# Spreading the loads of u's rows over time and fixing SyncE's order in the stage of u

## The chip, the cores and the metric

The kernel runs on one core of a Trainium2 chip. The metric is the device time of one execution in microseconds (us), lower is better. It is given as the median of several runs; beside it stands one execution that was recorded by the hardware profiler, with the times of every instruction and DMA.

Engines are named as in the profile: PE (matmul), DVE (VectorE), ACT (ScalarE), POOL (GpSimd) and SP (SyncE, which here does nothing but issue DMAs). Each works through its own instructions in order.

## The reference

One layer of a streaming encoder, on a sequence of 1024 tokens with 1024 channels, all in float32. The case lies in its first sub-layer, where the normalised input is projected into q, k, v, u and two gates, and u goes through a state-space branch:

```python
h = rms_norm(x, norm_mix_pre[l])
proj = h @ w_in[l]
q, k, v, u, gate_logits = jnp.split(proj, splits, axis=-1)
gate_attn, gate_ssm = jnp.split(jax.nn.sigmoid(gate_logits + b_gate[l]), 2, axis=-1)
o_attn = stick_breaking_attention(q, k, v)
o_ssm = s5_branch(u, ssm_a_re[l], ssm_a_im[l], ssm_log_dt[l], ...)
merged = gate_attn * (o_attn @ w_branch_attn[l]) + gate_ssm * (o_ssm @ w_branch_ssm[l])
x = x + rms_norm(merged @ w_out[l], norm_mix_post[l])
...
```

In `s5_branch` the 512 channels of u form 32 groups of 16, each with 64 complex states, and a linear recurrence runs over the 1024 tokens. Behind the first sub-layer come a cross-attention into 256 memory tokens and a gated feed-forward layer with a short convolution; they are the larger part of the kernel and the change doesn't touch them.

## The kernel before

**Precision.** A float32 matmul is made of three: each operand is split into a high part (a cast on ACT) and a low part (the difference). `mm3` (lines 143 to 145) multiplies high by high, high by low and low by high, so line 145 needs the low part of the weights.

**An order by hand.** From line 223 on, the first sub-layer is written against an own clock in us: `at(t, go)` puts a piece of work into a heap, and `all_events` runs the heap in order of time. The instructions of PE, ACT, DVE and POOL are emitted under `manual_schedule`, so each of these four engines has exactly that order. SP is not among them: its DMAs are placed by the scheduler of the tile framework, which is free to issue one before others that were written ahead of it.

**Semaphores of SP's DMAs.** The framework deals eight semaphores in turn to the DMAs of SP. A DMA waits until the one eight places before it has landed, so at most eight are under way. A wait is made by SP before it issues, and everything behind in its queue stands still meanwhile.

**The stage of u.** `channels` computes u transposed in four blocks b of 128 channels, each in two halves h of 512 tokens. DVE scales each half into the tile `ut` (line 482), and after the second half SP writes it to DRAM (`u_d`, line 484). The scan needs u with eight successive tokens and 16 channels on the 128 partitions, so the block is read back by eight small DMAs, one for each m, into 16 partitions of the tile `U` (line 488, 64 KB each). Before the change, all eight stand in one event, 4.0 behind the block's last matmul.

**The scan steps.** Then eight steps n run, `SLOT` = 12.2 apart; step n reads u's block n // 2. `states` is a matmul with `U` (line 766) and a chain on DVE (lines 775 to 787) that ends with `rc`; `outputs` multiplies `U` with the table `Tt` (line 800) and `rc` with `F1` (line 801). `Tt` has one buffer, and each block's entries are spread into it by eight DMAs from `ktt` (line 742). ACT applies the GELU to the sum (line 806). `tables` (lines 694 to 703) makes sines and cosines for a block: a memset on POOL, sums on DVE, then three activations on ACT.

**The filler.** Between these small pieces PE works on gate projections (`gate_job`, 16 steps of three matmuls for each). Their weights come by `Job.weights`: SP loads `ws` (line 253, two buffers), ACT casts it to `wh` (line 257), and the low part is either a difference on DVE (line 261, first job) or, from the second job on, made by ACT writing -`ws` into `wl` (line 265) and a DMA of POOL's queue that adds the weights from DRAM (line 266). A result half is copied by ACT into `glog` (line 295), which has one buffer in this stage, and SP writes it to DRAM (`g_d`, line 296). ACT can't copy the next half until that write has landed.

`u_begin` and `u_end` are the times of the plan at which the stage of u begins and at which the last matmuls of u end; `in_line` doesn't exist yet.

Of the kernel before, what the change touches and what calls it, by code (L numbers as in the profile page):

```python
# [20 lines left out]
P = 128  # L21
# [24 lines left out]
def kernel(ctx: ExitStack, tc: tile.TileContext, a: dict, out: bass.AP, dbg=None):  # L46
    nc = tc.nc
    V, G, C, T = nc.vector, nc.gpsimd, nc.scalar, nc.tensor
    dma = nc.sync.dma_start
# [7 lines left out]
    u_d = dpool.tile([512, 8, P], F32, name="u_d")  # L57
# [45 lines left out]
    def ps(tag):  # L103
        pool, w, n = psum[tag]
        return pool.tile([P, w], F32, tag=tag, name="ps_" + tag, bufs=n)
# [36 lines left out]
    def mm3(acc, sh, sl, mh, ml, first, last):  # L142
        T.matmul(acc, sh, mh, start=first, stop=False)  # L143
        T.matmul(acc, sh, ml, start=False, stop=False)  # L144
        T.matmul(acc, sl, mh, start=False, stop=last)  # L145
# [80 lines left out]
    STEP = 0.70  # L226
    events, seen = [], []

    def at(t, go):
        heapq.heappush(events, (t, len(seen), go))  # L230
        seen.append(t)
# [12 lines left out]
    class Job:  # L244
# [6 lines left out]
        def load(self, t):  # L251
            self.ws = wpool.tile([P, 1024], F32, tag="ws", name="ws", bufs=WS)
            dma(self.ws[:, :self.n], self.src)
# [90 lines left out]
    def h_hi(k, sl):  # L344
        return hT[0][k // 4][:, k % 4, sl]

    def h_lo(k, sl):
        return hT[1][k // 4][:, k % 4, sl]
# [16 lines left out]
    U = pa.tile([P, 32, P], F32, name="U")  # L365
# [97 lines left out]
        at(now + STEP + 7.0, put)  # L463

    ut = {}

    def channels(now, b, h, k):

        if k == 0:
            accs_[b, h] = ps("m")  # L470
        acc = accs_[b, h]
        ws = slice((k % 2) * 512 + b * P, (k % 2) * 512 + (b + 1) * P)
        wh, wl = (w[:, ws] for w in pair[1, k // 2])
        sl = slice(h * 512, (h + 1) * 512)
        mm3(acc, wh, wl, h_hi(k, sl), h_lo(k, sl), k == 0, k == KT - 1)
        if k < KT - 1:
            return

        def put(t):
            if h == 0:  # L480
                ut[b] = px.tile([P, 8, P], F32, tag="wr", name="ut", bufs=4)
            V.tensor_tensor(ut[b][:, :, 64 * h:64 * h + 64], acc.rearrange("p (j m) -> p m j", m=8), row_u[:, h], op=ALU.mult)
            if h:
                dma(u_d[b * P:(b + 1) * P], ut[b])

        def load(t):
            for m in range(8):
                dma(U[16 * m:16 * m + 16, 8 * b:8 * b + 8], u_d[b * P:(b + 1) * P, m].rearrange("(g c) j -> c g j", c=16))

        at(now + STEP + 0.2 + (1.4 if (b, h) == (0, 0) else 0.0), put)  # L490
        if h:
            at(now + STEP + 4.0, load)

    line(0.0, (lambda: x_load(0, 0), 0), (lambda: dma(gcol, a["g_cols"]), 0), (lambda: w_load(0, 0), 0),
         (lambda: x_load(1, 0), 0), (lambda: w_load(0, 1), 0), (lambda: dma(sp, a["ssm_p"]), 0), (lambda: x_load(0, 1), 0),
# [26 lines left out]
    def begin_of(t):  # L522
        return FIRST + 16 * STEP + 8 * STEP * (t - 2)

    u_begin = begin_of(KT)
# [314 lines left out]
    for t in range(2, KT):  # L840
        last_v = clock
        for k in range(KT):
            pe(STEP, tokens, 0, t, k)
    at(u_begin + 8.0, lambda _: open_t())
    steady = [lambda t, b=b, h=h, k=k: channels(t, b, h, k) for b in range(4) for h in range(2) for k in range(KT)]
    u_begin = clock
    for c in range(4):
# [3 lines left out]
    u_end = u_begin + 64 * STEP + 4.0  # L851
# [44 lines left out]
    def plan(t, took, go, n):  # L896
        heapq.heappush(timed, (t, len(seen), took, go, n))
        seen.append(t)

    plan(u_begin + 27.0, 1.75, intra, 0)  # L900
    plan(u_end - 8.0, 0.45, flip_w, 0)
    plan(u_end - 6.5, 0.45, flip_w, 1)
    plan(u_begin + 1.3, 0.15, lambda now, n: rows_of_rates(now, rates_x[:, 0], KT, rx_d, 0), 0)
# [4 lines left out]
    while timed:  # L908
        t0, _, took, go, n = heapq.heappop(timed)
# [51 lines left out]
    def glu_job(m):  # L961
        def out(t, h, sl, acc):
            def put(t):
                if h == 0:
                    og[m] = open_g.pool.tile([P, S], F32, tag="og", name="og", bufs=2)
                C.activation(og[m][:, sl], acc, AF.Sigmoid, bias=bglu[:, m:m + 1])

            def gated(t):
                V.tensor_tensor(og[m][:, sl], og[m][:, sl], yT[m][:, sl], op=ALU.mult)
                if h:  # L970
                    dma(os_d[m], og[m])

            at(t, put)
            at(t + 0.8, gated)

        return Job(a["w_glu_T"][m], out, n=512, steps=4, operand=lambda k, sl: (yh[k][:, sl], yl[k][:, sl]))

    clock = max(clock, g0_ + 5.2)
    for m in range(4):
        j = glu_job(m)  # L980
# [165 lines left out]
    t, nf, begun, last_z = 0.0, 0, {}, 1e9  # L1146
# [393 lines left out]
    for n, (ch, go, args, last) in enumerate(steady):  # L1540
        while timed and timed[0][0] <= clock + STEP / 2:
            _, _, took, turn_, x = heapq.heappop(timed)
# [17 lines left out]
    while timed:  # L1560
        _, _, took, turn_, x = heapq.heappop(timed)
# [1022 lines left out]
```

## Time and profile before

| | |
|---|---|
| median of 3 runs | 1646.17 us (1645.4 to 1646.4) |
| the profiled execution | 1641.96 us |
| its span, first to last instruction | 1640.2 us |
| mean granted TensorE clock | 0.998 |
| DMA, whole span | 287.13 MB, mean 175 GB/s |

The page gives each engine's busy time over the span. Its time line gives, for every instruction, start, duration, engine, line, operation and operands; in brackets stands how long the engine was idle before it, and what ended the idle time. A matmul is busy longer than it holds up the next one, since matmuls overlap, so the pace of PE is read from the starts. For SP a row is the issue of a DMA, which ends long before the data have landed.

### The profile page before, as it was taken

Reading aid. Unit: us, or ns where it says so; the run is one execution under the profiler, and the core shown is the slowest. Engines: PE = TensorE matmul, PEld = TensorE weight load, DVE = VectorE, ACT = ScalarE, POOL = GpSimd, SP = SyncE. Lnnn points to the kernel's source line nnn. Section 1 sums busy time; section 2 is a strip of 40 time slices with the busy share of each in tenths; the row PEclk is TensorE's granted clock in tenths of the full one; section 3 lists DMA queues with packets and bytes.
Section 4 is the critical chain, followed back from the end, with each engine's and each line's share of the span. In section 5 each row is a group of like instructions: output and inputs, shape, how many; then the busy total and the mean of one; then the engine's idle time right before and its main releaser. Section 6 shows DMA issues by size and latency. Waiting matters only on the chain.

```text
span 1640.2 us, 22339 instructions
## 1 busy us (share of the span) xinstructions
PE 1619.7 (99%) x7996; PEld 1361.3 (83%) x7996; DVE 1161.3 (71%) x1613; ACT 877.6 (54%) x1450; POOL 212.1 (13%) x307
## 2 busy tenths in 40 slices
PE   9999999999999999999999999999999999999998
PEld 7888888888888888888888888888888888888886
DVE  7888637676866688467555678988877888775473
ACT  5416346676766544345444556655555565654441
POOL 5000003333332000011000011111111111000010
PEclk9999999999999999999999999999999999999999
DMA  9444343232424954464413575777776767688571
GB/s 333 163 106 128 98 155 96 65 103 84 125 85 139 335 188 135 167 219 154 141 65 129 206 256 195 220 221 206 198 201 188 203 187 193 205 321 276 194 243 77
DMA packets 130340, 287.13 MB, mean 175 GB/s; under 512 B 22954, under 2 KB 31668, under 8 KB 130100
## 3 DMA queue, kind: packets, MB, share of 16 engines
q1 hardware_dynamic: 116644, 255.02, 46.2%
q0 software_dynamic: 10224, 21.24, 7.3%
q10 hardware_dynamic: 3360, 9.44, 1.5%
q8 instruction: 63, 1.03, 0.3%
q14 instruction: 49, 0.40, 0.1%
HBM read 209.74 MB, written 69.47 MB: 170 GB/s over the span
## 4 chain that ended last, share of the span: by engine, by line
PE 88%; issue 4%; DVE 3%; DMA 2%; ACT 2%; POOL 0%; SPq 0%; ACTq 0%; DVEq 0%; POOLq 0%
PE ps_p L1957 8%; PE ps_p L1958 8%; PE ps_p L1956 8%; PE ps_f L143 6%; PE ps_f L145 6%; PE ps_f L144 6%; PE ps_d L2429 4%; PE ps_d L2430 4%; PE ps_d L2431 4%; PE ps_m L143 3%; PE ps_m L144 3%; PE ps_m L145 3%; PE ps_o L1103 2%; PE ps_w L1078 2%; PE ps_z L143 1%
## 5 line engine op out<-in xcount | busy, mean ns | idle before, releaser
L143 PE MATMUL ps_f<-hT,wh 128*128 128x512 f32 x384 | 161.2, 420 | 0.0
L145 PE MATMUL ps_f<-hT,wl 128*128 128x512 f32 x384 | 150.9, 393 | 1.6 <-DMA wl<-in_w_in_T 1.6
L144 PE MATMUL ps_f<-hT,wh 128*128 128x512 f32 x384 | 150.6, 392 | 0.0
L1958 PE MATMUL ps_p<-qS,bm 128*128 128x512 f32 (+2 forms) x360 | 138.9, 386 | 0.6 <-DVE bm L2162 0.6
L1956 PE MATMUL ps_p<-qS,bm 128*128 128x512 f32 (+2 forms) x360 | 139.0, 386 | 0.1
L1957 PE MATMUL ps_p<-qS,bm 128*128 128x512 f32 (+2 forms) x360 | 138.8, 386 | 0.1
L149 DVE TENSOR_TENSOR dn<-raw,dn 128x1024 fp32r<-128x1024 f32 x77 | 93.4, 1223 | 62.9 <-ACT dn L148 60.2
L148 ACT CAST dn<-raw 128x1024 fp32r<-128x1024 f32 x77 | 80.5, 1054 | 87.1 <-PE ps_d L2431 38.0
L2429 PE MATMUL ps_d<-dn 128*128 128x512 f32 x308 | 119.8, 389 | 0.0
L2430 PE MATMUL ps_d<-dn 128*128 128x512 f32 x308 | 119.8, 389 | 0.0
L2431 PE MATMUL ps_d<-dn 128*128 128x512 f32 x308 | 119.8, 389 | 0.0
L1064 POOL TENSOR_TENSOR s<-s,s 128x127 f32<-128x127 f32 (+4 forms) x96 | 90.0, 938 | 220.3 <-DVE s L1058 175.0
L1957 PE MATMUL ps_p<-qA,bm 128*128 128x512 f32 (+2 forms) x272 | 104.5, 384 | 0.0
L1956 PE MATMUL ps_p<-qA,bm 128*128 128x512 f32 (+2 forms) x272 | 104.5, 384 | 0.0
L1958 PE MATMUL ps_p<-qA,bm 128*128 128x512 f32 (+2 forms) x272 | 104.5, 384 | 0.0
L1973 ACT COPY uu<-ps_p 128x512 f32<-128x512 f32 (+2 forms) x90 | 51.5, 573 | 93.0 <-PE ps_p L1958 93.0
L1902 POOL DMA_DIRECT2D bm<-in_ffn_up_T x61 | 53.5, 876 | 349.7 <-ACT bm L1901 168.5
L145 PEld LDWEIGHTS ps_f<-hT,wl 128*128 128x128 f32 x384 | 72.1, 188 | 18.2 <-DMA wl<-in_w_in_T 2.1
L1052 ACT ACTIVATE s<-ps_z,rates_x 128x128 f32<-128x128 f32 (+3 forms) x96 | 56.3, 587 | 53.6 <-PE ps_z L1041 48.1
L1958 PEld LDWEIGHTS ps_p<-qS,bm 128*128 128x128 f32 x360 | 67.6, 188 | 14.6 <-DVE bm L2162 1.2
L1956 PEld LDWEIGHTS ps_p<-qS,bm 128*128 128x128 f32 x360 | 67.6, 188 | 14.1 <-issue 0.8
L1957 PEld LDWEIGHTS ps_p<-qS,bm 128*128 128x128 f32 x360 | 67.6, 188 | 13.6 <-DVE qS L1784 0.2
(584 smaller groups left out, 4422.6 us busy)
## 6 DMA issues: line engine op xcount, KB each, us to landing
raw<-sd SPq DMA_DIRECT2D x77, 256.0 KB, 3.8
bm<-in_ffn_up_T POOLq DMA_DIRECT2D x61, 256.0 KB, 5.4
ws<-in_w_in_T SPq DMA_DIRECT2D x24, 512.0 KB, 3.6
ws<-in_xa_wo_N SPq DMA_DIRECT2D x23, 512.0 KB, 4.0
wv<-in_ffn_up_T SPq DMA_DIRECT2D x22, 512.0 KB, 4.0
dr<-in_ffn_down SPq DMA_DIRECT2D x22, 512.0 KB, 6.7
td<-st SPq DMA_DIRECT2D x44, 256.0 KB, 5.6
sd<-st SPq DMA_DIRECT2D x44, 256.0 KB, 3.4
```

The lines of the kernel that those rows point to most:

```text
L143: T.matmul(acc, sh, mh, start=first, stop=False)
L144: T.matmul(acc, sh, ml, start=False, stop=False)
L145: T.matmul(acc, sl, mh, start=False, stop=last)
L148: C.copy(dh, src)
L149: (lo or V).tensor_tensor(dl, src, f(dh), op=ALU.subtract)
L1064: G.tensor_tensor(s1[:, n0:e], s1[:, n0:e], s2[:, n0 + 1:e + 1], op=ALU.mult)
L1956: T.matmul(acc, bm[:, 0, ks], q[:, 0, k, cols], start=alone and k == 0, stop=False, skip_group_check=True)
L1957: T.matmul(acc, bm[:, 0, ks], q[:, 1, k, cols], start=False, stop=False, skip_group_check=True)
L1958: T.matmul(acc, bm[:, 1, ks], q[:, 0, k, cols], start=False, stop=k == 3, skip_group_check=True)
L2429: T.matmul(acc[i], v[:, 0, 0, sl], v[:, 0, 1], start=first, stop=False, skip_group_check=True)
L2430: T.matmul(acc[i], v[:, 0, 0, sl], v[:, 1, 1], start=False, stop=False, skip_group_check=True)
L2431: T.matmul(acc[i], v[:, 1, 0, sl], v[:, 0, 1], start=False, stop=last, skip_group_check=True)
```

## The change

The eight loads of a block are now eight events. A table, `LOAD_U`, gives for each block the time of the first one and the distance between them: 0.9, 1.2 and 2.0 us for the first three blocks, and for the last one 3.0 us, starting 16 us behind its matmuls. From 2 us behind `u_begin` to 44 us behind `u_end`, SP is put under `manual_schedule` as well, so in that stretch it issues its DMAs in the order in which they are written down.

```diff
     ut = {}
+    LOAD_U = (4.5, 0.9), (4.5, 1.2), (4.5, 2.0), (16.0, 3.0)
...
-        def load(t):
-            for m in range(8):
-                dma(U[16 * m:16 * m + 16, 8 * b:8 * b + 8], u_d[b * P:(b + 1) * P, m].rearrange("(g c) j -> c g j", c=16))
+        def load(t, m):
+            dma(U[16 * m:16 * m + 16, 8 * b:8 * b + 8], u_d[b * P:(b + 1) * P, m].rearrange("(g c) j -> c g j", c=16))
...
         if h:
-            at(now + STEP + 4.0, load)
+            for m in range(8):
+                at(now + STEP + LOAD_U[b][0] + LOAD_U[b][1] * m, lambda t, m=m: load(t, m))
...
     plan(u_begin + 27.0, 1.75, intra, 0)
+    in_line = ExitStack()
+    at(u_begin + 2.0, lambda _: in_line.enter_context(tc.manual_schedule(engines={mybir.EngineType.SP})))
+    at(u_end + 44.0, lambda _: in_line.close())
```

On PE, ACT, DVE and POOL every instruction stands where it stood. On SP the order changes between the last writes of v and the third spread of `Tt`; nothing is added or left out there. Three places matter. Line numbers of the changed kernel are up to four higher.

The first is SP's queue around the write of u's last block (`u_d<-ut`), the first spread of `Tt` and the first write of a gate half (`g_d<-glog`). Before, from that write of `u_d` on:

```order
L484 DMA u_d<-ut 128x1024
L488 DMA U<-u_d 16x8x128 x8
L742 DMA Tt<-ktt 16x128
L742 DMA Tt<-ktt 32x128
L742 DMA Tt<-ktt 48x128
L742 DMA Tt<-ktt 64x128
L742 DMA Tt<-ktt 80x128
L742 DMA Tt<-ktt 96x128
L742 DMA Tt<-ktt 112x128
L742 DMA Tt<-ktt 128x128
L488 DMA U<-u_d 16x8x128 x8
L296 DMA g_d<-glog 128x512
```

And now, from the same write:

```order
L485 DMA u_d<-ut 128x1024
L488 DMA U<-u_d 16x8x128
L743 DMA Tt<-ktt 16x128
L743 DMA Tt<-ktt 32x128
L743 DMA Tt<-ktt 48x128
L743 DMA Tt<-ktt 64x128
L743 DMA Tt<-ktt 80x128
L743 DMA Tt<-ktt 96x128
L743 DMA Tt<-ktt 112x128
L743 DMA Tt<-ktt 128x128
L488 DMA U<-u_d 16x8x128 x2
L296 DMA g_d<-glog 128x512
```

One load of u stands ahead of `Tt` in place of eight, and three ahead of the write of `g_d` in place of sixteen.

The second place is SP's queue from the last writes of v through the first blocks of u, where the weights of the first two gate jobs (`ws<-in_w_in_T`) are loaded. Before:

```order
L461 DMA v_d<-vr 128x512
L253 DMA ws<-in_w_in_T 128x1024 x2
L461 DMA v_d<-vr 128x512 x2
L423 DMA rx_d<-row_k 8x128
L461 DMA v_d<-vr 128x512
L425 DMA U<-rx_d 128x1024
L484 DMA u_d<-ut 128x1024
L488 DMA U<-u_d 16x8x128 x8
```

Now these two loads stand behind the second and the third write of `u_d`; the rows begin at the second:

```order
L485 DMA u_d<-ut 128x1024
L488 DMA U<-u_d 16x8x128 x7
L253 DMA ws<-in_w_in_T 128x1024
L488 DMA U<-u_d 16x8x128
L485 DMA u_d<-ut 128x1024
L423 DMA rm_d<-row_k 2x128
L488 DMA U<-u_d 16x8x128
L253 DMA ws<-in_w_in_T 128x1024
L488 DMA U<-u_d 16x8x128 x3
```

The first of the two has moved behind seven loads of u's second block, the second behind the write of the third block and its first load.

The third place is SP's queue from the reload of `row_k` on, with the weights of the third job and of those behind it. Before:

```order
L286 DMA row_k<-rx_d 128x512
L253 DMA ws<-in_w_in_T 128x1024
L296 DMA g_d<-glog 128x512
L253 DMA ws<-in_w_in_T 128x1024
L296 DMA g_d<-glog 128x512
L253 DMA ws<-in_w_in_T 128x1024
L742 DMA Tt<-ktt 16x128
```

And now:

```order
L286 DMA row_k<-rx_d 128x512
L296 DMA g_d<-glog 128x512
L253 DMA ws<-in_w_in_T 128x1024
L488 DMA U<-u_d 16x8x128 x3
L296 DMA g_d<-glog 128x512
L488 DMA U<-u_d 16x8x128 x2
L253 DMA ws<-in_w_in_T 128x1024
L743 DMA Tt<-ktt 16x128
```

The third job's load has moved behind the second write of `g_d`, the fourth job's behind the third, and the fifth job's behind the second spread of `Tt`, which is out of these rows.

## Prediction, made before the changed kernel ran

> **What bounds the kernel now.** I read the page first: its head and the engines' busy time.
>
> ```profile
> span 1640.2 us, 22339 instructions
> PE 1619.7 (99%) x7996; PEld 1361.3 (83%) x7996; DVE 1161.3 (71%) x1613; ACT 877.6 (54%) x1450; POOL 212.1 (13%) x307
> ```
>
> PE is idle for 1640.2 - 1619.7 = 20.5 us of the whole span. The change adds and removes no arithmetic, so all it can give is some of these 20.5 us. The second view is PE's waits, cut to 60 to 240 us, the stretch in which the moved transfers run.
>
> ```profile
> PE ps_f L145 <- DMA wl<-in_w_in_T: 1.6, 1, 1.6
> PE ps_m L800 <- issue: 0.4, 1, 0.4
> ```
>
> There are two waits in it. The time line of PE shows them, with neighbours that give the normal pace and the times used further down. A row is start, duration, engine, line, operation.
>
> ```profile
> 112.40 0.39 PE L145 MATMUL ps_f<-hT,wl 128*128 128x512 f32 x1
> ...
> 115.12 0.39 PE L145 MATMUL ps_f<-hT,wl 128*128 128x512 f32 x1
> 115.92 0.46 PE L800 MATMUL ps_m<-Tt,U 128*128 128x128 f32 x2 [0.41 <-issue]
> ...
> 117.56 0.39 PE L801 MATMUL ps_m<-F,rc 128*128 128x128 f32 x2
> ...
> 123.02 0.39 PE L145 MATMUL ps_f<-hT,wl 128*128 128x512 f32 x1
> ...
> 133.41 0.40 PE L144 MATMUL ps_f<-hT,wh 128*128 128x512 f32 x1
> 135.45 0.50 PE L145 MATMUL ps_f<-hT,wl 128*128 128x512 f32 x1 [1.64 <-DMA wl<-in_w_in_T]
> ...
> 142.83 0.39 PE L801 MATMUL ps_m<-F,rc 128*128 128x128 f32 x2
> ```
>
> One matmul takes 0.39 us but the next starts 0.23 us after it (112.40 to 115.12 is twelve such steps of 0.227). So line 800 would have started at 115.12 + 0.23 = 115.35 and started at 115.92: **0.57 us lost**. Line 145 would have started at 133.41 + 0.23 = 133.64 and started at 135.45: **1.81 us lost**. The idle figures in the brackets (0.41 and 1.64, 2.05 together) leave out the overlap of two matmuls; by starts it is 2.38.
>
> What made them late is SP's queue, which issues in order. Its time line:
>
> ```profile
> 43.34 0.94 SPq L253 DMA_DIRECT2D ws<-in_w_in_T  x2
> ...
> 81.50 3.64 SPq L488 DMA_DIRECT2D U<-u_d  x8
> ...
> 91.45 0.34 SPq L484 DMA_DIRECT2D u_d<-ut  x1
> ...
> 101.76 0.34 SPq L484 DMA_DIRECT2D u_d<-ut  x1
> 102.19 6.81 SPq L488 DMA_DIRECT2D U<-u_d  x8
> 109.10 5.08 SPq L742 DMA_DIRECT2D Tt<-ktt  x8
> 114.22 3.90 SPq L488 DMA_DIRECT2D U<-u_d  x8
> 118.22 0.38 SPq L296 DMA_DIRECT2D g_d<-glog  x1
> ...
> 119.11 0.45 SPq L253 DMA_DIRECT2D ws<-in_w_in_T  x1
> ```
>
> Three bursts of eight stand in a row. The eight of Tt start at 109.10, behind eight of U, and are out at 109.10 + 5.08 = 114.18; line 800 waits for them. The first write of g_d waits behind all 24, until 118.22. It holds the only buffer of glog, and ACT needs that buffer back:
>
> ```profile
> 98.08 1.06 ACT L257 CAST wh<-ws 128x1024 fp32r<-128x1024 f32 x1 [0.32 <-PE ps_m L144]
> ...
> 121.46 0.59 ACT L295 COPY glog<-ps_f 128x512 f32<-128x512 f32 x1 [14.40 <-DMA g_d<-glog]
> ...
> 126.31 0.60 ACT L806 ACTIVATE y<-ps_m 128x512 f32<-128x512 f32 x1
> ...
> 127.74 0.59 ACT L295 COPY glog<-ps_f 128x512 f32<-128x512 f32 x1
> 128.21 1.07 ACT L265 ACTIVATE wl<-ws 128x1024 fp32r<-128x1024 f32 x1
> ```
>
> ACT stands still for 14.40 us and then works off its queue; the wl of the third gate job is ready at 128.21 + 1.07 = 129.28. Only then can POOL issue the transfer that adds to it:
>
> ```profile
> 100.41 1.06 POOL L266 DMA_DIRECT2D wl<-in_w_in_T  x1 [5.29 <-ACT wl L265]
> ...
> 129.59 0.88 POOL L266 DMA_DIRECT2D wl<-in_w_in_T  x1 [27.92 <-DVE F L725]
> ```
>
> It lands 5.8 us later, and PE has waited from 133.64.
>
> **The change part by part.** No instruction of PE, ACT, DVE or POOL changes place. SP issues the same DMAs in another order. I need times from issue to landing: minimum, median and maximum by tile (wl from 95 to 150 us, ws from 40 to 150, g_d from 100 to 150), then the one u_d write issued in the quiet stretch from 90 to 100 and the one from 95 to 150:
>
> ```profile
> DMA to landing us min/median/max: 5.3/5.8/7.9
> ...
> DMA to landing us min/median/max: 4.1/4.9/5.7
> ...
> DMA to landing us min/median/max: 2.0/3.1/3.5
> ...
> u_d<-ut SPq DMA_DIRECT2D x1, 512.0 KB, 2.6
> ...
> u_d<-ut SPq DMA_DIRECT2D x1, 512.0 KB, 5.4
> ```
>
> *Tt earlier.* Behind the u_d write at 101.76 stands now one load of U, then the eight of Tt. At the 5.08 / 8 = 0.635 us that each took, they are issued from 102.6 to 107.7; each DMA also waits for the one eight places before it, and for the seventh that is the u_d write itself, landed at 104.4 to 107.2. So all eight are out by 107.0 to 108.5. Line 800 wants them at 115.35 and was 0.57 late with 114.18: over 5 us earlier is enough. The **0.57 us go**. Its partner, line 801, needs rc, which the DVE rows below give at 113.75 + 0.69 = 114.44, still in time.
>
> *g_d earlier.* Two loads of U follow, then the first g_d write, at 108.3 to 109.3, landing after 2.0 to 3.5: 110.3 to 112.8. The second half of the first gate job ends on PE at 112.40 + 0.39 = 112.79. So ACT's second glog copy waits for PE alone, at about 112.8 in place of 121.46. Before, 4.85 us lay between this copy and line 806 (121.46 to 126.31), so line 806 comes at 117.7; its input, the group of line 800, is there at 117.56 + 0.39 - 0.57 = 117.4. The ws of the third job is issued behind the second g_d write, at 114.0 in place of 119.11, and lands at 118.1 to 119.7. wh then ends at 119.2 to 120.7. The third glog copy waits for PE: 123.02 + 0.39 - 0.57 = 122.8. wl follows, from 123.4 to 124.5; POOL issues at 124.8 (0.31 behind ACT, as before) and the landing is at 130.1 to 132.7. PE now wants it at 133.64 - 0.57 = 133.07. Even the longest landing fits, so the **1.81 us go**.
>
> *Two weight loads later.* The ws of the first two gate jobs were issued at 43.34, far ahead. The first now stands behind seven loads of u's second block, at 81.50 + 3.64 = 85.1 at the latest. ACT's cast of it lies before the one of 98.08: it ended at 98.08 - 0.32 = 97.76 and began 1.06 earlier, at 96.7; 85.1 + 5.7 = 90.8 is in time. The second stands behind the u_d write of 91.45 and one load: 91.45 + 2.6 + 0.5 = 94.6, landing at 98.7 to 100.3. ACT's cast, at 98.08 before, moves to 98.7 to 100.3, the POOL transfer of 100.41 to 101.0 to 102.6, and it lands by 110.5 at worst; PE wants it three steps behind 112.40, at 113.1. But a memset of x stands behind it on POOL, and DVE's table work behind that:
>
> ```profile
> 101.64 2.37 DVE L697 TENSOR_TENSOR x<-x,turns 128x8 f32<-128x8 f32 x7
> ...
> 107.37 0.69 DVE L775 TENSOR_TENSOR bp<-ps_m,cosT 128x512 f32<-128x512 f32 x1 [1.36 <-PE ps_m L766]
> ...
> 113.75 0.69 DVE L787 TENSOR_TENSOR rc<-rc,bt 128x508 f32<-128x508 f32 x1
> ...
> 128.76 0.69 DVE L725 TENSOR_TENSOR F<-F,tq 128x512 f32<-128x512 f32 x1
> 130.62 2.38 DVE L697 TENSOR_TENSOR x<-x,turns 128x8 f32<-128x8 f32 x7 [1.17 <-POOL rc L783]
> ...
> 134.91 0.68 DVE L775 TENSOR_TENSOR bp<-ps_m,cosT 128x512 f32<-128x512 f32 x1
> ...
> 141.28 0.69 DVE L787 TENSOR_TENSOR rc<-rc,bt 128x508 f32<-128x508 f32 x1
> ```
>
> DVE has 1.36 us to spare before bp, and rc is 115.35 + 0.23 - 114.44 = 1.1 us early for line 801. A delay of up to 2.5 us is covered; mine is 0.6 to 2.2. Cost: **nothing**, and 1 us for 1 us beyond a cast at 100.5.
>
> *What is late next.* The second wait of DVE for POOL (1.17 at 130.62) goes as well, since POOL's queue is free sooner, and all before it comes 0.57 earlier: x at 128.9, bp 4.29 behind, rc 6.37 + 0.69 behind that: 140.2. Line 801 wants rc at 142.83 - 2.38 = 140.45. That is the tightest spot, 0.2 us to spare; between nothing and 0.3 us could come back here, and I take nothing. The loads of u's last block, now spread behind the second block's Tt loads, are out eleven issues of 0.635 behind 133.41 at the latest, at 140.4; the scan step that reads them is four steps of 12.2 (SLOT in the kernel) behind the one of 134.91, at 183. The Tt loads of the second block wait for PE's last read of Tt, before and after, so they move with PE.
>
> **Sum.** 0.57 + 1.81 = 2.38 us (2.05 by idle time alone). The profiled execution took 1641.96 us, 1640.2 of span and 1.8 around it: 1639.6. The runs have a median of 1646.17, 4.2 above that one execution; I take the same difference off: **1643.8 us**, 0.14% faster, which is under the 0.2% (3.3 us) that a measurement of this kernel can tell from no change.
>
> **The rivals.**
> *The second wait stays.* The row of 129.59 names DVE's F, not ACT, as what released POOL. If POOL truly waits for DVE there, wl is issued at about 129 as before and only 0.57 goes: 1645.6. Against it: at 100.41, where POOL's row names ACT, ACT's product ends 1.07 behind the cast of 98.08 + 1.06, at 100.2, and POOL issues 0.2 later; here it issues 0.31 behind ACT's end, about the same. The Trainium skill, page "SBUF — State Buffer", section "SBUF: two separate sides", states that a transfer issued by GpSimd can be held while VectorE runs an operation in a two-port mode, since the descriptors cannot be written then. By that rule the time would be this rival's, 1645.6. The same page's section "Who interferes with whom" gives the tensor_tensor form, which F is, no such mode, so the row bears the rule out poorly. Other ways of being late by over 0.4 us on that chain end between 1644 and 1645.6. Chance together 0.12.
> *Slower: the second weight load becomes the wait.* It now starts behind a u_d write. If that write lands like the busy one (5.4) and ws at its longest (5.7), the cast comes at 91.45 + 5.4 + 0.5 + 5.7 = 103.0, 2.5 us past the point of decision at 100.5, and line 801 waits 2.5 us. The 0.57 is lost in it; if the second wait goes all the same the time is 1646.17 + 2.5 - 2.38 = 1646.3, and if it stays, 1648.1. For it: rc and DVE's x stand close, as the rows show. Against it: in that stretch the queue carries nothing but u, and the write at 91.45 took 2.6. Chance 0.07.
> *More than the sum.* Some of the other 18 us of PE's idle time lie later; PE, 2.4 us ahead, may meet a few better or worse. Two us either way: 1641.8 or 1645.8. Chance of the good side 0.13.
>
> **How the numbers follow.** The forecast itself (1643.3 to 1644.5) has 0.68. Faster by over 0.2% means under 1642.9: most of the third rival and a little of the forecast's scatter, 0.15. Slower by over 0.2% means over 1649.5, which needs more than the second rival's upper end: 0.05. The rest, 0.80, is within 0.2%. The range goes from the third rival's good end to the middle of the slower one: 1641.8 to 1647.0.
>
> **What would show it.** Right: no wait of PE at the Tt matmul near 115.4 nor at line 145 near 133; the second glog copy on ACT at about 113, ended by PE; the first g_d write issued before 110; the third wl transfer near 125. Wrong: a cast later than 100.5 with a PE wait for rc at about 116; a POOL transfer still at 129; a PE wait of a few tenths near 140.5 would be the rc of the third scan step. If all of these are right and the time differs by more than 1 us, the cause lies after 240 us.

## The result, and the profile after

| | before | after |
|---|---|---|
| median | 1646.07 us (1643.89 to 1646.97, 7 runs) | 1640.49 us (1639.37 to 1642.26, 7 runs) |
| the profiled execution, span | 1641.96, 1640.2 | 1640.49, 1638.7 |
| ratio, 95% interval | | 0.9965 (0.9955 to 0.9975) |

The changed kernel is 5.6 us faster (4.1 to 7.4 by the interval). Foretold were 2.4 us; the time lies below the range. The two profiled executions differ by only 1.5 us. That contrast is the question of this section: 1.5 between two profiles, 5.6 between the medians.

The page of the changed kernel, and the waits of PE from 60 to 240 us (total, times, longest):

```profile
span 1638.7 us, 22339 instructions
PE 1618.8 (99%) x7996; PEld 1360.5 (83%) x7996; DVE 1160.8 (71%) x1613; ACT 878.0 (54%) x1450; POOL 212.0 (13%) x307
```

```profile
PE ps_f L145 <- DMA wl<-in_w_in_T: 0.3, 1, 0.3
```

The wait at the `Tt` matmul is gone and the one at line 145 has shrunk from 1.6 to 0.3 us. PE's time line at the three places (start, duration):

```profile
114.47 0.39 PE L145 MATMUL ps_f<-hT,wl 128*128 128x512 f32 x1
114.69 0.38 PE L801 MATMUL ps_m<-Tt,U 128*128 128x128 f32 x2
...
131.78 0.47 PE L143 MATMUL ps_f<-hT,wh 128*128 128x512 f32 x1
132.10 0.40 PE L144 MATMUL ps_f<-hT,wh 128*128 128x512 f32 x1
132.84 0.50 PE L145 MATMUL ps_f<-hT,wl 128*128 128x512 f32 x1 [0.35 <-DMA wl<-in_w_in_T]
...
140.25 0.39 PE L802 MATMUL ps_m<-F,rc 128*128 128x128 f32 x2
```

Line 801 (800 before) follows line 145 at the normal distance, 0.22 us. SP's queue, then ACT's and POOL's:

```profile
101.11 0.34 SPq L485 DMA_DIRECT2D u_d<-ut  x1
101.49 0.46 SPq L488 DMA_DIRECT2D U<-u_d  x1
102.04 7.63 SPq L743 DMA_DIRECT2D Tt<-ktt  x8
109.72 1.06 SPq L488 DMA_DIRECT2D U<-u_d  x2
110.88 0.38 SPq L296 DMA_DIRECT2D g_d<-glog  x1
...
114.36 0.43 SPq L253 DMA_DIRECT2D ws<-in_w_in_T  x1
```

```profile
97.73 1.05 ACT L257 CAST wh<-ws 128x1024 fp32r<-128x1024 f32 x1 [0.61 <-DMA ws<-in_w_in_T]
...
113.36 0.59 ACT L295 COPY glog<-ps_f 128x512 f32<-128x512 f32 x1 [6.95 <-DMA g_d<-glog]
...
122.61 1.06 ACT L265 ACTIVATE wl<-ws 128x1024 fp32r<-128x1024 f32 x1
```

```profile
123.98 0.88 POOL L266 DMA_DIRECT2D wl<-in_w_in_T  x1 [22.65 <-ACT wl L265]
```

ACT gets `glog` back at 113.36 in place of 121.46, and the third `wl` transfer is issued at 123.98 in place of 129.59. The chain moved in the foretold direction and to about the foretold end, but two of the signs named for a right prediction are not there. The eight DMAs of `Tt` take 7.63 us to issue, not 5.08, so the first write of `g_d` is issued at 110.88, not before 110, and ACT's second copy is ended by that write (6.95 us of waiting), not by PE; it starts at 113.36, not at 112.8. DVE's chain of the third scan step, called the tightest spot with 0.2 us to spare, has 140.25 - 138.69 - 0.69 = 0.87:

```profile
138.69 0.69 DVE L788 TENSOR_TENSOR rc<-rc,bt 128x508 f32<-128x508 f32 x1
```

### The profile page after: what moved, and what is told of

The parts are those of the page before. It is cut to its first block, busy times and chain, and to the rows that moved or that the text cites. A ratio compares the mean times of both kernels' runs of the same rounds, so it can differ in the third digit from the quotient of the medians.

```text
span 1638.7 us, 22339 instructions
## 1 busy us (share of the span) xinstructions
PE 1618.8 (99%) x7996; PEld 1360.5 (83%) x7996; DVE 1160.8 (71%) x1613; ACT 878.0 (54%) x1450; POOL 212.0 (13%) x307
## 4 chain that ended last, share of the span: by engine, by line
PE 87%; DVE 4%; DMA 3%; issue 3%; ACT 2%; POOL 0%; SPq 0%; ACTq 0%; DVEq 0%; POOLq 0%
PE ps_p L1962 8%; PE ps_p L1961 8%; PE ps_p L1960 8%; PE ps_f L143 6%; PE ps_f L145 6%; PE ps_f L144 6%; PE ps_d L2433 4%; PE ps_d L2434 4%; PE ps_d L2435 4%; PE ps_m L145 3%; PE ps_m L143 3%; PE ps_m L144 3%; PE ps_o L1107 2%; PE ps_w L1082 2%; PE ps_z L143 1%
```

## The experiments

### Both kernels recorded again

Two copies, unchanged, with runs of their own. First the kernel before:

> The kernel before, unchanged, recorded once more. The changed kernel was 5.6 us faster by medians (1640.49 against 1646.07), but only 1.5 us by the two recorded executions (1640.49 against 1641.96). Theory L (the recorded execution of before was a lucky one): a second recording takes 1645 to 1647, with PE idle 4 us longer than in the first one, and the place of these 4 us shows where the change gains. Theory R (recording itself makes before faster, or its runs scatter without a place): the second recording is near 1642 again.

Measured: 1645.82 us (10 runs), ratio to the kernel before 0.9999 (0.9988 to 1.0010). Its PE time line from 131 us on:

```profile
131.71 0.48 PE L143 MATMUL ps_f<-hT,wh 128*128 128x512 f32 x1
132.02 0.40 PE L144 MATMUL ps_f<-hT,wh 128*128 128x512 f32 x1
135.67 0.50 PE L145 MATMUL ps_f<-hT,wl 128*128 128x512 f32 x1 [3.25 <-DMA wl<-in_w_in_T]
...
136.53 0.63 PE L145 MATMUL ps_f<-hT,wl 128*128 128x512 f32 x1
...
139.09 0.63 PE L145 MATMUL ps_f<-hT,wl 128*128 128x512 f32 x1
139.51 0.53 PE L143 MATMUL ps_f<-hT,wh 128*128 128x512 f32 x1
139.89 0.39 PE L144 MATMUL ps_f<-hT,wh 128*128 128x512 f32 x1
```

Two things differ from the first recording. The wait is 3.25 us, not 1.64. And behind it the matmuls take 0.63 us and start 0.43 apart for over 3 us, in place of 0.39 and 0.23. The windows of the same stretch tell why. Columns: window, length, then busy time and count of PE, PEld, DVE, ACT and POOL, then the granted clock, the DMA share and GB/s.

```profile
134.00:136.00 2.00, 0.33 (x1) 0.30 (x2) 1.94 (x4) 1.97 (x3) 0.00 (x0) 1.00 0.62 164
136.00:138.00 2.00, 2.00 (x7) 1.56 (x6) 1.93 (x6) 2.00 (x3) 0.00 (x0) 0.60 0.30 111
138.00:140.00 2.00, 2.00 (x7) 1.57 (x6) 1.94 (x4) 0.99 (x2) 0.00 (x0) 0.55 0.00 0
140.00:142.00 2.00, 2.00 (x11) 1.64 (x10) 1.97 (x4) 0.00 (x0) 0.00 (x0) 1.00 0.00 0
```

PE counts as fully busy in both middle windows, but with 7 matmuls each in place of 11: the granted clock fell to 0.60 and 0.55. The eleven steps from 135.67 to 139.89 took 4.22 us. In the first recording, where the clock stayed at 1.00 behind this wait, they took 2.63. So here the wait costs its own 135.67 - 132.02 - 0.23 = 3.42 us and **1.59 us more behind it**, which no view of waits lists.

The changed kernel:

> The changed kernel, unchanged, recorded once more, on the same chip as the second recording of before. Theory L: 1639.5 to 1642.5, with the same waits of PE as in its first recording (no wait at the Tt matmul, 0 to 0.4 us at the wl of the third gate job), so that the two recordings of this chip differ by 4 to 6 us. Theory R: they differ by 1.5 to 2.5 us again.

Measured: 1642.22 us (10 runs), ratio 0.9975 (0.9964 to 0.9987), so 4.1 us (2.1 to 5.9). No `Tt` wait, and 0.6 us at one line 145, this time of the fourth gate job (148.17).

### The two halves of the change

The spread of the loads alone (`LOAD_U` and eight events, without the manual order of SP):

```diff
+    LOAD_U = (4.5, 0.9), (4.5, 1.2), (4.5, 2.0), (16.0, 3.0)
...
-            at(now + STEP + 4.0, load)
+            for m in range(8):
+                at(now + STEP + LOAD_U[b][0] + LOAD_U[b][1] * m, lambda t, m=m: load(t, m))
```

> The loads of u's rows spread over time as in the change, but SP's order left to the scheduler. The two weight loads then stay early, ws of the first two jobs, and two loads of u stand ahead of the first spread of Tt in place of eight; the ws of the third job stands behind the second write of g_d, as in the change. Theory S (the gain comes from breaking up the bursts of eight): all or nearly all of the gain, 1640 to 1642. Theory O (the stated order of SP is what gains): 1644 to 1646.

Measured: 1641.53 us (12 runs), 0.9970 (0.9960 to 0.9979).

The order alone, with bursts of eight:

```diff
+    in_line = ExitStack()
+    at(u_begin + 2.0, lambda _: in_line.enter_context(tc.manual_schedule(engines={mybir.EngineType.SP})))
+    at(u_end + 44.0, lambda _: in_line.close())
```

> SP's order stated as in the change, but the loads of u's rows left in bursts of eight. The eight Tt DMAs stand ahead of all loads of u's third block's... no: behind the third block's eight loads, which now stand before the last write of u_d, so Tt stands directly behind that write; the first write of g_d stands behind eight loads in place of sixteen. Theory S: at most the 0.57 us of the Tt wait and part of the 1.81 us of the wl wait, 1644 to 1646. Theory O: all of the gain, 1640 to 1642.

Measured: 1642.74 us (12 runs), 0.9977 (0.9967 to 0.9988). Their gains, 4.8 and 3.6 us by medians against 4.1 for the whole change beside them, can't be told apart by these intervals; the order alone lies between the ranges of both theories. So each half alone brings most of the gain, and the two don't add up. Either one leaves fewer loads of U ahead of the first `Tt` spread and of the first write of `g_d`, which is issued at 110.28 with the spread alone and at 112.97 with the order alone (eight loads still stand ahead of it there), in place of 118.22. The third `wl` is issued at 124.0 and at 125.3.

The order alone also shows the rival that the prediction called slower. Its second `ws` stands behind eight loads of U. ACT's cast, DVE's table work and PE's line 801 in this kernel:

```profile
101.10 1.05 ACT L257 CAST wh<-ws 128x1024 fp32r<-128x1024 f32 x1 [4.20 <-DMA ws<-in_w_in_T]
...
104.66 2.38 DVE L697 TENSOR_TENSOR x<-x,turns 128x8 f32<-128x8 f32 x7 [3.78 <-POOL rc L783]
...
116.15 0.46 PE L801 MATMUL ps_m<-F,rc 128*128 128x128 f32 x2 [1.27 <-DVE rc L787]
```

This recording runs 0.85 us ahead of the first one of before here (its third write of `u_d` is issued at 90.60, there at 91.45), so the point of decision, 100.5, lies at 99.65. The cast is 1.45 us past it, and line 801, which by the pace of its neighbours would have started some 0.22 behind 114.49, is 1.44 late, with 1.27 of it idle. In the changed kernel the cast starts at 97.73, and PE doesn't wait there.

### The kernel before, twice more

> The kernel before, recorded a third time. Theory W: the landing of the wl transfer of the third gate job takes 7 to 8.5 us and PE waits 2.5 to 4 us near 133; where the wait is over 3 us the granted clock falls behind it to about 0.6. Rival L (the first recording, with a landing of 5.8 us and a wait of 1.6 us, is the usual case): 5.5 to 6.5 us, wait 1.3 to 2.3, clock 1.00.

> The kernel before, recorded a fourth time. Theory W and rival L expect the same as for the third recording.

Measured: waits of 2.76 and 2.94 us, both with the fall of the clock, although both are under the 3 us that theory W asked for. The four recordings of before and two of after, with the stretch from the first line 143 of the third job (two rows above the wait) to the first line 817 (818 after) behind 155 us:

| | wl issued | landing after | wait of PE | clock falls behind it | stretch |
|---|---|---|---|---|---|
| before, first | 129.59 | 5.8 | 1.64 | no | 25.16 |
| before, second | 128.08 | 7.5 | 3.25 | yes | 28.37 |
| before, third | 128.53 | 7.3 | 2.76 | yes | 27.90 |
| before, fourth | 127.88 | 7.5 | 2.94 | yes | 28.05 |
| after, first | 123.98 | 8.8 | 0.35 | no | 24.07 |
| after, second | 123.61 | 8.3 | none | no | 24.13 |

The first recording's times lie about 1 us later than the others', so its issue at 129.59 isn't late by comparison; the landing is what differs. The recording on which the prediction rests is the odd one of four. Its 1641.96 us lie below every run of before in the comparisons, whose lowest is 1642.42.

### One write of g_d less, in the kernel before

This kernel leaves out the first write of `g_d` behind the bursts; that half of `g_d` gets another job's values later.

```diff
-                dma(g_d[gi][:, sl], gt)
+                if (gi, h) != (EARLY_SSM[0], 0):
+                    dma(g_d[gi][:, sl], gt)
+                if (gi, h) == (EARLY_SSM[1], 1):
+                    dma(g_d[EARLY_SSM[0]][:, :512], gt)
```

> The kernel before, without the first write of g_d behind the bursts; that half of g_d is written later, from the buffer of another job, so its contents are not the reference's. The bursts of U and Tt stay. Theory W (the time lies in the chain g_d write, second glog copy, ACT's queue, wl, and what PE's wait for that wl brings with it): ACT's second glog copy comes at about 113, ended by PE; wl's transfer is issued at 124 to 126 in place of 128 to 129.6; PE waits 0 to 0.6 us near 133 in place of 1.6 to 3.3; the wait for Tt near 115.5 stays (0.3 to 0.6 us). Time 1641.3 to 1643, as for the changed kernel. Rival X (the bursts cost by themselves, through traffic or through PE's wait for Tt, or the gain lies behind 240 us): the time stays within 1 us of the kernel before, 1645 to 1647, although the wait near 133 is gone.

Measured: 1645.81 us (12 runs), 1.0002 (0.9992 to 1.0012). The time is what rival X foretold, but not for X's reason. The third `wl` is issued at 125.87 and its wait is gone, as theory W had it. PE waits at another place instead, for the `wl` of the fourth job. ACT, POOL, PE and the windows behind:

```profile
134.45 0.59 ACT L295 COPY glog<-ps_f 128x512 f32<-128x512 f32 x1 [4.44 <-DMA g_d<-glog]
```

```profile
144.01 0.87 POOL L266 DMA_DIRECT2D wl<-in_w_in_T  x1 [17.11 <-ACT wl L265]
```

```profile
152.07 0.80 PE L145 MATMUL ps_f<-hT,wl 128*128 128x512 f32 x1 [3.67 <-DMA wl<-in_w_in_T]
```

```profile
150.00:152.00 2.00, 0.00 (x0) 0.00 (x0) 1.97 (x5) 0.00 (x0) 0.00 (x0) 0.97 0.35 114
152.00:154.00 2.00, 1.93 (x5) 1.45 (x6) 0.66 (x1) 0.00 (x0) 0.00 (x0) 0.50 0.04 12
154.00:156.00 2.00, 2.00 (x11) 1.77 (x10) 0.00 (x0) 0.59 (x1) 0.00 (x0) 0.68 0.00 0
```

It is the same chain one round later. The scheduler, free on SP here, put a write of `g_d` into the middle of the second `Tt` spread. ACT waits 4.44 us for the buffer and from there on is busy without a pause until it makes the fourth `wl`, which comes late, and PE, which is now ahead, pays 3.67 us and a fall of the clock. So this run does not part W from X by its time. It shows that removing one wait of this chain is worth nothing if the next round of it is as late.

### A late wl in the changed kernel

Only ACT's `wl` of the third job is moved, behind two copies of E; on POOL a memset of x then comes ahead of its transfer. SP, PE and DVE keep the order of the changed kernel.

```diff
-                first_of[ns].weights(clock, *((3.8, 2.7) if ns == 64 else (10.2, 9.1, True)))
+                first_of[ns].weights(clock, *((3.8, 2.7) if ns == 64 else (10.2, 5.0 if ns == 96 else 9.1, True)))
```

> The changed kernel with one thing put back: ACT makes the wl of the third gate job behind its two copies of E in place of ahead of them, and POOL issues the transfer at about 128.2 (memset of x first) in place of 124. The order of SP, PE and DVE stays that of the changed kernel, no burst comes back. Theory W: PE waits at line 145 near 133 until the transfer lands, at 128.2 + 5.3 to 8.5 = 133.5 to 136.7, so 0.4 to 3.5 us; with a wait of 3 us or more the granted clock falls behind it to about 0.6 for some 3 us (1.5 us more). Time 1643 to 1647, 1 to 5 us over the changed kernel. Rival X (bursts, or something behind 240 us): the wait is there or not, but the time stays within 0.7 us of the changed kernel, 1641 to 1642.5.

Measured: 1641.48 us (11 runs), 0.9979 (0.9970 to 0.9988). That lies inside the range of rival X and below the 1643 to 1647 of theory W, though the wait that W named is there. POOL's issue, the landing, PE and the window behind:

```profile
127.77 0.88 POOL L266 DMA_DIRECT2D wl<-in_w_in_T  x1 [13.36 <-DVE x L698]
```

```profile
133.44 0.50 PE L145 MATMUL ps_f<-hT,wl 128*128 128x512 f32 x1 [1.46 <-DMA wl<-in_w_in_T]
```

```profile
134.00:136.00 2.00, 2.00 (x10) 1.67 (x9) 1.97 (x5) 1.97 (x3) 0.00 (x0) 1.00 0.62 197
```

The transfer is issued when the kernel before issues it, but lands after 5.6 us, with the `Tt` burst beside it. The wait is 1.46 us, the clock stays at 1.00, and the stretch of the table is 24.96 us, 0.9 over the changed kernel. So an issue at 128 alone doesn't cost 4 us. Two things could: a longer landing, or a still later issue. The next two runs try one each.

**A ws load beside it.** As the run with the late `wl`, and the `ws` load that needs the buffer which ACT's `wl` frees stands ahead of the `Tt` spread, as in the kernel before:

```diff
-        def weights(self, t0, hi=5.0, lo=3.8, added=False):
+        def weights(self, t0, hi=5.0, lo=3.8, added=False, lead=9.0):
-            for dt_, go in ((9.0 + hi, self.load), (hi, self.high), (lo, self.low_added if added else self.low)):
+            for dt_, go in ((lead + hi, self.load), (hi, self.high), (lo, self.low_added if added else self.low)):
...
-                first_of[ns].weights(clock, *((3.8, 2.7) if ns == 64 else (10.2, 9.1, True)))
+                first_of[ns].weights(clock, *((3.8, 2.7) if ns == 64 else (10.2, 5.0 if ns == 96 else 9.1, True, 26.0 if ns == 128 else 9.0)))
```

> As the run with the late wl, but the ws load that needs the buffer which ACT's wl frees stands on SP directly ahead of the second spread of Tt, as in the kernel before, so that it starts within about 0.3 us of the wl transfer (127.8). Theory N (a ws load of 512 KB started beside it makes the wl transfer land after 7 to 7.6 us instead of 5.3 to 5.8): landing at about 135.1, PE waits 2.8 to 3.3 us at line 145 in place of 1.5, the granted clock falls to 0.5 to 0.6 for some 3 us behind the wait and matmuls take 0.63 us (1.5 us more), time 1644 to 1646. Rival B (the spread of Tt beside it, or mere scatter, sets the landing): landing 5.3 to 5.8 as in the run with the late wl, wait about 1.5, clock 1.00, time 1641 to 1642.3.

Measured: 1646.06 us (11 runs), 1.0002 (0.9993 to 1.0011). SP, POOL, the time to landing of that one transfer, PE and the windows:

```profile
127.67 0.35 SPq L253 DMA_DIRECT2D ws<-in_w_in_T  x1
128.35 6.06 SPq L743 DMA_DIRECT2D Tt<-ktt  x8
```

```profile
127.95 0.88 POOL L266 DMA_DIRECT2D wl<-in_w_in_T  x1 [12.35 <-DVE x L698]
```

```profile
DMA to landing us min/median/max: 8.3/8.3/8.3
```

```profile
136.29 0.79 PE L145 MATMUL ps_f<-hT,wl 128*128 128x512 f32 x1 [4.14 <-DMA wl<-in_w_in_T]
```

```profile
134.00:136.00 2.00, 0.00 (x0) 0.00 (x0) 1.93 (x6) 1.97 (x3) 0.00 (x0) 0.59 0.58 155
136.00:138.00 2.00, 1.71 (x4) 1.42 (x5) 1.94 (x4) 2.00 (x3) 0.00 (x0) 0.50 0.51 165
138.00:140.00 2.00, 2.00 (x6) 1.52 (x6) 1.97 (x4) 0.56 (x1) 0.00 (x0) 0.50 0.12 34
140.00:142.00 2.00, 2.00 (x8) 1.57 (x7) 0.95 (x2) 0.00 (x0) 0.00 (x0) 0.71 0.00 0
```

Theory N holds, by more than it said: the issue is 0.2 us later, the `Tt` burst beside it is the same, and 512 KB of `ws` started 0.3 us ahead lengthen the landing from 5.6 to 8.3 us. The wait is 4.14, the clock falls to half, and the whole gain of the change is gone. One recording each could be scatter, but the other traces sort the same way. Where no `ws` load is issued within 4 us of the third `wl` it lands after 5.3 (one write less), 5.5 (spread alone), 5.6 and 5.7 us; where one is issued within 0.3 us of it and takes the usual time to issue, after 7.3 to 8.8 us, in six recordings. With the order alone, where it is issued 0.87 us ahead, the landing takes 6.5.

**A later wl, without a ws beside it.** ACT's `wl` stands behind its y as well (`3.0` in place of `5.0` in the diff of the late `wl`):

> As the run with the late wl, but ACT makes the wl of the third gate job also behind its y, about 2.4 us later; no ws load comes beside the transfer. Transfer issued at about 130.2, landing 5.3 to 5.8 later at 135.5 to 136, PE waits 3.4 to 4.1 us. Theory W with the clock (a wait of 2.8 us or more lets the granted clock fall to 0.5 to 0.6 for some 3 us, 1.5 us more): stage from the first matmul of line 732 to line 818 about 80.5 us, time 1644.5 to 1646.5. Rival M (only the wait counts, or the loss is made up later): stage 78.5 to 79.2, time 1642.5 to 1644.

Measured: 1646.27 us (11 runs), 1.0004 (0.9995 to 1.0013), inside the range of theory W with the clock and outside that of rival M. The landing takes 5.7 us, the wait is 4.05, and the stretch is 29.10 us in place of 24.96 with the late `wl`:

```profile
136.37 0.79 PE L145 MATMUL ps_f<-hT,wl 128*128 128x512 f32 x1 [4.05 <-DMA wl<-in_w_in_T]
```

```profile
136.00:138.00 2.00, 1.63 (x4) 1.34 (x5) 1.94 (x5) 2.00 (x3) 0.00 (x0) 0.56 0.77 238
138.00:140.00 2.00, 2.00 (x7) 1.57 (x6) 1.97 (x4) 0.72 (x1) 0.00 (x0) 0.59 0.00 0
```

The stage from line 732 to line 818 is 81.3 us (160.70 - 79.38), 0.8 over what theory W said and further over rival M's 78.5 to 79.2. So with U's loads still spread, and here with SP's new order untouched, one late transfer brings back the time of the kernel before, by either road. The waits of 4.05 and 4.14 are longer than the 2.76 to 3.25 of the kernel before, so the two runs show what a late `wl` can cost, not that it is the same sum.

## Why the prediction was wrong

**Right: the path.** Burst of U, late write of `g_d`, ACT without its buffer, late `wl`, PE. Its end moved as foretold: `wh` at 119.91 (foretold 119.2 to 120.7), the third `wl` on POOL at 123.98 (124.8). Its middle was off: `Tt` took longer to issue, the write of `g_d` came at 110.88 (108.3 to 109.3), and ACT's copy waited for it; the range given for `wh` was wide enough to take that in. The transfer landed after 8.8 us, longer than the 7.9 taken as the longest, and so 0.51 us of the wait (132.84 - 132.10 - 0.23) stayed. The runs with a late `wl` show that this transfer alone can undo the gain. The rival that POOL waits for DVE there is out: POOL's row of 123.98 names ACT, and so do the rows of the third and fourth recordings of before (128.53 and 127.88).

**Right: the first term.** The 0.57 us at the `Tt` matmul went.

**Right: the covers.** Neither the two `ws` loads that moved back nor the third rc became a wait in the changed kernel, and the run with the order alone shows that the first of these was a real danger with its point of decision in the right place (1.45 us past it, 1.44 late).

**Wrong: the size of the second term, 1.81 us.** "It lands 5.8 us later, and PE has waited from 133.64" took the landing of one transfer in one recording for the usual one. The three other recordings land after 7.3 to 7.5 us. By starts, as in the prediction, they lose 3.42, 2.93 (135.88 - 132.72 - 0.23) and 3.11 us (135.40 - 132.06 - 0.23). The same trace held the warning: 5.8 stood in a row of three with a longest of 7.9. The prediction used that longest for the transfer of the changed kernel, to see whether it would still be in time, and not for that of the kernel before.

**Missing: what follows a long wait.** Behind these waits the clock falls, and the matmuls lose another 1.6 us (1.59 above; in the third recording 27.90 - 25.16 - (2.93 - 1.81) = 1.62). The sum put this at nothing. Behind the 1.64 us of the first recording nothing of it is to be seen, but that recording did hold one such fall at its very start, behind a wait of 1.91 us (shown under the clock below).

**Wrong: from one execution to the median.** "I take the same difference off" supposed that whatever made that execution 4.2 us shorter than the median was outside the change. It was mostly in it. The stretch was 25.16 us where the other three have a median of 28.05, so 2.9 of the 4.2 us were this very wait being short.

**The sum put right.** With the median of the four recordings, 27.98, against 24.10 for the two of after, the stretch gives 3.9 us. With the 0.57 of the `Tt` wait that is 4.5, inside both measured intervals (4.1 to 7.4 and 2.1 to 5.9). A typical late `wl` alone would give 3.1 + 1.6 + 0.57 = 5.3 us. But the changed kernel keeps 0.5 or 0.7 us by starts at the third or the fourth `wl`, for which PE now comes earlier, and one of the four recordings of before is the short one. What remains to the 5.6 of the first comparison, 1.1 us, is below what these runs can settle. Behind the stretch the recordings of one and the same kernel differ by up to 2 us, and no experiment aimed there. One part of that can be seen: in the second recording of the changed kernel the granted clock is 0.64 and 0.50 in the windows from 1004 to 1008, behind two waits of 0.57 and 1.11 us; in the first, which has such waits too, it stays at 1.00.

**Open.** Why the first recording's landing was short is read, not shown. There the `ws` load beside the transfer took 1.44 us to issue (the row of 129.31 on SP, where such rows otherwise take 0.33 to 0.45), so its data probably started after those of `wl`. The two late `wl` runs that differ in a `ws` load show that such a load lengthens the landing, not that its delay shortened it there. A version of the changed kernel that keeps `ws` loads away from both the third and the fourth `wl` could win the 0.5 to 0.7 us that are left; it was not tried. (The spread alone happens to keep one away from the third, and there it doesn't wait, but then waits 0.92 us for the fourth.)

## What to carry to other kernels

A wait taken from one recording is a sample: look at the spread of what ends it in the same trace, and if the recorded execution lies off the median by more than the gain you compute, ask first whether the difference is the wait itself. A long wait of PE can cost more than its length, so compare the granted clock and the number of matmuls per window behind it with those ahead; busy time and waits don't show it. And when a wait in a repeating chain goes, look at the next round of the chain before counting the gain.

## What the runs showed of the hardware

**The clock.** At the third and fourth `wl`, waits of 1.46 and 1.64 us left the granted clock at 1.00, and waits of 2.76, 2.94, 3.25, 3.67, 4.05 and 4.14 us were each followed by a fall to half. This is no border that holds by length alone. At the start of the kernel the first recording of before waits 1.91 us and the clock falls; the run with the later `wl` waits 2.21 us and it doesn't. The row and a window of each, first the recording of before:

```profile
10.02 0.51 PE L143 MATMUL ps_m<-wh,hT 128*128 128x512 f32 x1 [1.91 <-ACT hT L439]
12.00:14.00 2.00, 2.00 (x7) 1.55 (x6) 2.00 (x3) 1.53 (x3) 2.00 (x1) 0.50 1.02 418
```

```profile
10.36 0.50 PE L143 MATMUL ps_m<-wh,hT 128*128 128x512 f32 x1 [2.21 <-ACT hT L439]
12.00:14.00 2.00, 2.00 (x11) 1.57 (x10) 2.00 (x4) 1.19 (x2) 2.00 (x1) 1.00 1.02 416
```

The run with the `ws` beside it has a fall even behind 1.47 us (at 7.31; clock 0.51 and 0.63 in the windows from 8 to 12). So between about 1.5 and 2.2 us it went either way here, and from 2.76 on it fell each time. The length of the fall can be worked out from the windows: a window of 2 us spent wholly at half clock shows 0.50, so its missing share times 2 / 0.5 is the time at half clock. In the second recording of before it is (0.40 + 0.45) x 2 / 0.5 = 3.4 us, with the later `wl` (0.44 + 0.41) x 2 / 0.5 = 3.4, and with the `ws` beside it (0.41 + 0.50 + 0.50 + 0.29) x 2 / 0.5 = 6.8, twice as long. It may begin while PE still waits (134 to 136 in the last case) or only after it has resumed (behind 136 in the second recording), so the price differs from run to run. By starts these two runs lose 4.22 and 4.31 us to the wait itself (136.37 - 131.92 - 0.23 and 136.29 - 131.75 - 0.23). Beyond that the stretch grows by 1.5 us with the later `wl` (29.10 - 25.16 - (4.22 - 1.81)) and by 2.3 with the `ws` beside it (29.93 - 25.16 - (4.31 - 1.81)). The Trainium skill, page "TensorE: Matmul & The Clock Gate", section "Part 1: The HAM clock gate (the "warmup" mystery)", tells of a clock that is either whole or half, set by an activity window of about 3.4 us that runs freely. Clocks down to 0.50 and no lower, and falls of 3.4 us and twice that, agree with the trace, and a window that runs freely would fit the scatter of the short waits. The same page's section "HAM oscillation — how this bites in real kernels" puts the rule as no idle gap over about 3.4 us; here 2.76 us of idle time were enough, and once 1.47, so by these runs that border is too high.

**Transfers of two queues.** The 512 KB of a `wl` transfer landed after 5.6 us with the `Tt` burst beside it and after 8.3 with a `ws` load of 512 KB besides. The Trainium skill, page "DMA: Bandwidth & Descriptors", section "Issuing engines are not separate DMA queues", states that transfers of all engines interleave on the same 16 DMA engines; the pair agrees.
